# A hybrid decoder layer on one core: the up projection computed by channels, with the weights as left operand and the norm's factor applied to its result

## The chip, the cores and the metric

The kernel runs on one core of one Trainium2 chip. The metric is the device time of one execution in microseconds (us): the median of three runs of the kernel before is 1485.3, and the runs lie between 1483.8 and 1486.86.

## The reference

One layer of a hybrid decoder trunk, for 256 tokens of width 2048, in float32. A state-space group and an attention group work side by side on a normalised input, their outputs go through one output projection, then come a feed-forward network with a convolution in it and a gated embedding. The part that the change touches is the feed-forward network:

```
n       = RMSNorm(h)                       # h / sqrt(mean(h^2) + 1e-6) * gain, per token
[g | u] = causal_dwconv3(n @ W_up)         # 2048 -> 2 x 5632 channels; 3 taps over tokens, per channel, and a bias
h       = h + (SiLU(g) * u) @ W_down       # 5632 -> 2048
h       = h + sigmoid(RMSNorm(h) @ W_pg) * RMSNorm(p @ W_pe)
```

The factor 1 / sqrt(mean(h^2) + 1e-6) is one number per token. It may be applied before or after the product with W_up, since it is the same for all channels; the convolution mixes tokens, so it comes behind the factor.

## The kernel before, in words

**Tiles.** The 256 tokens (T) are two blocks of 128 (NB = 2). Weights come in chunks of 512 output columns (NC = 512), and a chunk with its 2048 rows comes in eight pieces of two row tiles each (KW = 2; 128 x 1024 numbers, 512 KB), each with one DMA on SyncE's queue. `load_w` (L201) makes two tiles of each piece: wh, the high part, by a cast on ScalarE (L195), and wl = w - wh on VectorE (L196). Both are fp32r, the type that TensorE takes here. The activations are kept the same way, as high and low tiles (class `Lhs`, L240), with channels on the partitions. There are four buffers of wh and of wl.

**Products.** `products` (L214) computes, for a piece's two row tiles and the two token blocks, three matmuls each into the block's accumulator (a PSUM bank of 128 tokens x 512 channels): high activations by wh (L231), high by wl (L232), low by wh (L233). The activations are the left operand (the one that TensorE loads, 128 x 128), the weights stream past as the right operand, 512 columns a matmul. A chunk of the up projection has 16 row tiles x 2 blocks x 3 = 96 such matmuls.

**The up projection** (`up`, L781) handles one chunk: the 96 matmuls (`gemm`, L783), a copy of the two accumulators that is scaled by the norm's factor rh (one number per token, and so per partition; ScalarE, L787), and `conv_chunk` (L284). The convolution runs along tokens, so the chunk is first turned by eight transposes on TensorE (L291) into two PSUM tiles; from there `conv_tile` (L275) makes the last tap with the bias on ScalarE (L278) and adds the two others on VectorE (L280). There are 22 chunks, 11 of g and 11 of u, in turn. SiLU is on ScalarE, the product g * u on GpSimd (L803), and the split of the result on ScalarE and VectorE. The down projection (`project`, L382) of a segment of chunk pairs (segments of 2, 2, 2, 2, 2 and 1 pairs) comes one segment later.

**Ahead of it.** The last output projection (`project` with `next_lhs`, L747) adds its chunks to the residual h and at once prepares the next left operand hT: ScalarE squares and sums h (L374), and `transpose_split` (L257) turns h with 16 transposes a chunk (L264) into two PSUM tiles and writes the high part, times the norm's gain (gain: per channel), on ScalarE (L198) and the low part on VectorE (L199). `finish_rstd` (L377) sums the squares (L379) and makes rh with a multiply and add (L188) and a power on GpSimd (L190). Then the layer's embedding input pT and the convolution's weights fcw are loaded on ScalarE's queue (L756, L763), and pT is split into ph and pl (L764). hT uses the same SBUF tiles as the left operand aT before it.

**Behind it.** The last down projection prepares h2T in the same way (L810), then come the embedding product (L811) and the gate (L821 to L832).

**PSUM.** Three pools of two buffers each are open for the whole kernel: the accumulator pairs (ps_acc, 4 banks), the turned tiles (ps_tr, 2) and the rest (ps_ms, 2): all eight banks.

**What sets the order.** The program is written in the order above, but a list scheduler with a model of the engines reorders it: each engine gets its own stream of instructions, and runs it strictly in order. So a matmul that is written early may stand later in TensorE's stream, and in the streams transposes stand among the matmuls of the next step. The scheduler's choice is fixed when the kernel is built. A buffer is taken when its earlier readers are done; a pool that is opened in place of a closed one waits in the same way.

Of the kernel before, what the change touches and what calls it, by code (L numbers as in the profile page):

```python
# [11 lines left out]
F32 = mybir.dt.float32  # L12
F32R = mybir.dt.float32r
I32 = mybir.dt.int32
AF = mybir.ActivationFunctionType
ALU = mybir.AluOpType
AX = mybir.AxisListType
PSUM = bass.MemoryType.PSUM

P = 128  # L20
T = 256
# [4 lines left out]
NC = 512  # L26
# [38 lines left out]
def hybrid_layer(  # L65
# [29 lines left out]
    ps_acc = ctx.enter_context(tc.tile_pool(name="ps_acc", bufs=2, space=PSUM))  # L95
    ps_tr = ctx.enter_context(tc.tile_pool(name="ps_tr", bufs=2, space=PSUM))
    ps_ms = ctx.enter_context(tc.tile_pool(name="ps_ms", bufs=2, space=PSUM))
# [3 lines left out]
    def nm(s):  # L101
        uid[0] += 1
        return f"{s}_{uid[0]}"
# [15 lines left out]

    def acc_pair():  # L120
        return [ps_acc.tile([P, NC], F32, tag=f"acc{b}", name=nm(f"acc{b}")) for b in range(NB)]

    def tr_tile():
        return ps_tr.tile([P, NC], F32, tag="tr", name=nm("tr"))
# [115 lines left out]
    class Lhs:  # L240


        def __init__(self, pool, kt, tag):
            self.t = [
                (sb(pool, [P, KG, T], f"{tag}h{g}", F32R), sb(pool, [P, KG, T], f"{tag}l{g}", F32R))
                for g in range((kt + KG - 1) // KG)
            ]

        def part(self, k):
            h, l = self.t[k // KG]  # L250
            return h[:, k % KG, :], l[:, k % KG, :]

# [117 lines left out]
    def next_lhs(lhs, ss, n, gain):  # L370

        for b in range(NB):
            sq = sb(small, [P, NC], "hsq")
            S.activation(out=sq, in_=hres[b][:, n * NC : (n + 1) * NC], func=AF.Square, accum_out=ss[:, b, n : n + 1])  # L374
        transpose_split([hres[b][:, n * NC : (n + 1) * NC] for b in range(NB)], lhs, 4 * n, gain)
# [374 lines left out]
    mix.close()  # L750

# [27 lines left out]
    with tc.tile_pool(name="ffn", bufs=2) as fp:  # L779

        def up(c):  # L781
            acc = acc_pair()
            gemm(acc, hT, [w_up[c, g] for g in range(KT // KW)])  # L783
            t = []
            for b in range(NB):
                u_ = sb(fp, [P, NC], f"u{b}")
                S.activation(out=u_, in_=acc[b], func=AF.Copy, scale=rh[:, b : b + 1])  # L787
                t.append(u_)
            cv = sb(fp, [P, 4, T], f"cv{c // NPAIR}")
            conv_chunk(t, cv, fcw, 3, 4 * c)  # L790
            return cv
# [108 lines left out]
```

## Time and profile before

| what | value |
|---|---|
| median of three runs | 1485.3 us (1483.8 to 1486.86) |
| the profiled execution's own time | 1484.0 us |
| its span in the trace | 1482.3 us |
| TensorE, matmuls (PE) | 1472.4 us busy, 99% of the span |
| TensorE, weight loads (PEld) | 1199.1 us busy, 81% |
| VectorE (DVE) | 961.8 us busy, 65% |
| ScalarE (ACT) | 799.9 us busy, 54% |
| GpSimd (POOL) | 155.2 us busy, 10% |
| DMA | 271.65 MB, mean 183 GB/s |

How to read the profile's lines: a busy time is the time in which an engine had an instruction under way. Matmuls are pipelined, so two of them overlap, and their pace is read from their starts and not from their durations. A row of groups gives the program's line, the engine, the operation, the tiles (out<-in), shapes and count, then the sum in us and the mean of one in ns, then the idle time of the engine ahead of them and what ended it. A row of the timeline gives the start in us from the span's start, the duration in us, the engine, the line, the instruction with its tiles and shape, and a count where several follow each other; brackets behind it name a wait and what ended it. A row of windows gives a stretch and, for PE, PEld, DVE, ACT and POOL in that order, the busy time with the number of instructions (ahead of them, the sum of PE's), then the granted clock of TensorE, the share of DMA and the GB/s. A "q" behind an engine's name is its DMA queue.

### The profile page before, as it was taken

To read this page: it belongs to the slowest core of one execution; us is meant where nothing else is said; L and a number is where in the kernel's file an instruction comes from. 1 tells how busy PE (TensorE), PEld (TensorE's weight loads), DVE (VectorE), ACT (ScalarE), POOL (GpSimd) and SP (SyncE) were. 2 spreads that over 40 slices of the span, in tenths; PEclk is the share of its full clock that TensorE was granted. 3 is DMA by queue.
4 is the path that set the end of the run, shared out by engine and by line. 5 is a ranking of instruction groups with operands and counts; after the bars stand their busy time and mean duration, and the time that the engine had idled before them with its cause. 6 is when DMAs were issued, how large, how long until landed. Compare 5 with 4: busy or idle time off the path is not lost.

```text
span 1482.3 us, 18476 instructions
## 1 busy us (share of the span) xinstructions
PE 1472.4 (99%) x6836; PEld 1199.1 (81%) x6836; DVE 961.8 (65%) x1264; ACT 799.9 (54%) x1111; POOL 155.2 (10%) x148
## 2 busy tenths in 40 slices
PE   9999999999999999999999999999999999999998
PEld 7787888888777777788888888888888888888887
DVE  7578776656768687766556646565665556566854
ACT  7575555645555554566555545544543554454643
POOL 1004022034033030000000000000000000000000
PEclk9999999999999999999999999999999999999999
DMA  9665655655555555466666666666666665666673
GB/s 344 187 200 171 203 183 160 185 155 172 157 156 150 164 146 160 132 191 204 184 187 186 186 193 185 187 190 191 182 192 191 184 193 186 187 190 188 208 222 100
DMA packets 79098, 271.65 MB, mean 183 GB/s; under 512 B 8752, under 2 KB 11504, under 8 KB 78624
## 3 DMA queue, kind: packets, MB, share of 16 engines
q1 hardware_dynamic: 78176, 269.55, 59.8%
q8 instruction: 53, 0.87, 0.2%
q10 hardware_dynamic: 720, 0.74, 0.1%
q0 software_dynamic: 112, 0.19, 0.1%
q14 instruction: 37, 0.30, 0.1%
HBM read 268.32 MB, written 2.13 MB: 182 GB/s over the span
## 4 chain that ended last, share of the span: by engine, by line
PE 93%; DVE 2%; DMA 2%; POOL 2%; issue 1%; ACT 1%; SPq 0%; DVEq 0%; POOLq 0%
PE acc L231 26%; PE acc L232 26%; PE acc L233 26%; PE acc L223 5%; PE tr L291 2%; PE ms L656 1%; PE ms L505 1%; DMA seg<-scr 1%; PE ms L697 1%; PE tr L264 1%; PE tr L689 1%; DVE wl L196 1%; DMA w<-in_w_in_dram 1%; PE acc L330 1%; PE acc L331 1%
## 5 line engine op out<-in xcount | busy, mean ns | idle before, releaser
L196 DVE TENSOR_TENSOR wl<-w,wh 128x1024 fp32r<-128x1024 f32 (+1 forms) x493 | 616.5, 1253 | 406.8 <-ACT wh L195 405.1
L195 ACT CAST wh<-w 128x1024 fp32r<-128x1024 f32 (+1 forms) x493 | 516.8, 1050 | 484.7 <-PE acc L233 382.0
L232 PE MATMUL acc<-wl,ah 128*128 128x512 f32 x1168 | 457.1, 391 | 0.8 <-DVE wl L196 0.5
L231 PE MATMUL acc<-wh,ah 128*128 128x512 f32 x1168 | 457.5, 393 | 0.0
L233 PE MATMUL acc<-wh,al 128*128 128x512 f32 x1168 | 457.3, 393 | 0.0
L232 PEld LDWEIGHTS acc<-wl,ah 128*128 128x128 f32 x1168 | 219.4, 188 | 47.7 <-DVE wl L196 2.1
L231 PEld LDWEIGHTS acc<-wh,ah 128*128 128x128 f32 x1168 | 219.5, 188 | 45.7 <-issue 1.8
L233 PEld LDWEIGHTS acc<-wh,al 128*128 128x128 f32 x1168 | 219.0, 188 | 44.8 <-issue 0.8
L231 PE MATMUL acc<-wh,gh 128*128 128x512 f32 x352 | 137.5, 391 | 0.0
L233 PE MATMUL acc<-wh,gl 128*128 128x512 f32 x352 | 137.5, 391 | 0.0
L232 PE MATMUL acc<-wl,gh 128*128 128x512 f32 x352 | 137.1, 389 | 0.0
L803 POOL TENSOR_TENSOR cv<-cv,cv 128x1024 f32<-128x1024 f32 x11 | 35.8, 3254 | 648.4 <-DVE cv L280 562.8
L231 PE MATMUL acc<-wh,yh 128*128 128x512 f32 x256 | 101.1, 397 | 0.0
L232 PE MATMUL acc<-wl,yh 128*128 128x512 f32 x256 | 100.6, 393 | 0.0
L233 PE MATMUL acc<-wh,yl 128*128 128x512 f32 x256 | 100.5, 395 | 0.0
L280 DVE SCALAR_TENSOR_TENSOR cv<-tr,fcw,cv 128x254 f32<-128x254 f32 (+1 forms) x176 | 74.0, 475 | 19.3 <-ACT cv L278 19.3
L368 DVE TENSOR_TENSOR h<-h,acc 128x512 f32<-128x512 f32 x112 | 73.7, 680 | 11.1 <-PE acc L233 11.1
L233 PEld LDWEIGHTS acc<-wh,gl 128*128 128x128 f32 x352 | 66.1, 188 | 13.5
L232 PEld LDWEIGHTS acc<-wl,gh 128*128 128x128 f32 x352 | 66.1, 188 | 13.5
L231 PEld LDWEIGHTS acc<-wh,gh 128*128 128x128 f32 x352 | 66.1, 188 | 13.3
L278 ACT ACTIVATE cv<-tr,fcw 128x256 f32<-128x256 f32 x88 | 44.9, 561 | 34.1 <-PE tr L291 34.1
L231 PEld LDWEIGHTS acc<-wh,yh 128*128 128x128 f32 x256 | 48.1, 188 | 12.0 <-issue 2.1
(240 smaller groups left out, 1282.9 us busy)
## 6 DMA issues: line engine op xcount, KB each, us to landing
w<-in_w_up_dram SPq DMA_DIRECT2D x176, 512.0 KB, 3.9
w<-in_w_in_dram SPq DMA_DIRECT2D x127, 512.0 KB, 3.7
w<-in_w_down_dram SPq DMA_DIRECT2D x88, 512.0 KB, 3.7
w<-in_w_out_dram SPq DMA_DIRECT2D x64, 512.0 KB, 3.7
w<-in_w_pg_dram SPq DMA_DIRECT2D x32, 512.0 KB, 4.3
seg<-scr SPq DMA_DIRECT2D x8, 512.0 KB, 6.0
h<-in_x_dram SPq DMA_DIRECT2D x2, 1024.0 KB, 8.3
w<-in_w_pe_dram SPq DMA_DIRECT2D x4, 512.0 KB, 3.7
```

The source lines that it names most:

```text
L195: S.copy(hi, src)
L196: V.tensor_tensor(out=lo, in0=src, in1=hi.bitcast(F32), op=ALU.subtract)
L223: PE.matmul(acc[b], lhsT=l, rhs=r, start=(k == 0 and m == 0), stop=(k == total - 1 and m == 2))
L231: PE.matmul(acc[b], lhsT=hi, rhs=wh[:, i, :], start=(k == 0), stop=False)
L232: PE.matmul(acc[b], lhsT=hi, rhs=wl[:, i, :], start=False, stop=False)
L233: PE.matmul(acc[b], lhsT=lo, rhs=wh[:, i, :], start=False, stop=(k == total - 1))
L264: PE.transpose(tr[:, i, b * P : (b + 1) * P], src[b][:, f * P : (f + 1) * P], ident)
L278: S.activation(out=dst, in_=ps, func=AF.Identity, scale=taps[n - 1], bias=bias)
L280: V.scalar_tensor_tensor(out=dst[:, s:], in0=ps[:, : T - s], scalar=taps[n - 1 - s], in1=dst[:, s:], op0=ALU.mult, op1=ALU.add)
L291: PE.transpose(tr[:, i, b * P : (b + 1) * P], src[b][:, f * P : (f + 1) * P], ident)
L368: V.tensor_tensor(out=hs, in0=hs, in1=acc[b], op=ALU.add)
L803: G.tensor_tensor(out=cg, in0=cg, in1=cu, op=ALU.mult)
```

## The change

In words:

- **One PSUM pool from there on.** When rh has been made, the three pools are closed and one pool ps_b is opened, of four tags with two buffers each: again eight banks. `acc_pair` and `tr_tile` take their tiles from it in turn. The embedding, the gate and the down projection use it too.
- **High and low activations side by side.** `Lhs` now holds one tile for each group with the high 256 tokens and the low 256 next to each other, so that one right operand can span both (`pair`, 512 columns).
- **The up projection by channels.** `up` uses the weights as left operand: for each row tile and each of four groups of 128 channels, one long product, wh by the high and low activations (512 columns, L823 of the kernel after), and one short one, wl by the high activations (256 columns, L821). They go in rows of four, long then short, for the second row tile of a piece short then long. Each of the four banks holds 128 channels x 256 tokens of the high products in its left half (the wl products should land with one of the halves: they go to the right half, `acc[f][:, T:]`) and the low ones in its right half. A chunk has 64 long and 64 short products. Its result has channels on the partitions already, so the eight transposes of a chunk go.
- **The norm's factor behind the product.** rh has one number per token, and tokens now lie along a row. So rt, a tile of 128 partitions x 256 tokens with the factor in each partition, is made once by two matmuls with the identity (L803) and a copy (L804). For each chunk ScalarE copies the four left halves (L827), VectorE adds the four right halves (L828) and multiplies all four by rt in one instruction (L829). Then `conv_tile` works as before, from SBUF in place of PSUM.

The diff:

```diff
--- before
+++ after
@@ -92,9 +92,11 @@
     act = ctx.enter_context(tc.tile_pool(name="act", bufs=1))
     const = ctx.enter_context(tc.tile_pool(name="const", bufs=1))
     small = ctx.enter_context(tc.tile_pool(name="small", bufs=2))
-    ps_acc = ctx.enter_context(tc.tile_pool(name="ps_acc", bufs=2, space=PSUM))
-    ps_tr = ctx.enter_context(tc.tile_pool(name="ps_tr", bufs=2, space=PSUM))
-    ps_ms = ctx.enter_context(tc.tile_pool(name="ps_ms", bufs=2, space=PSUM))
+    banks = ExitStack()
+    ps_acc = banks.enter_context(tc.tile_pool(name="ps_acc", bufs=2, space=PSUM))
+    ps_tr = banks.enter_context(tc.tile_pool(name="ps_tr", bufs=2, space=PSUM))
+    ps_ms = banks.enter_context(tc.tile_pool(name="ps_ms", bufs=2, space=PSUM))
+    ps_b = []
 
     uid = [0]
 
@@ -117,10 +119,22 @@
         if n:
             G.memset(sb(pool, [P, n // 4], "fill", bufs=1), 0.0)
 
+    def bank(i):
+
+        return ps_b[0].tile([P, NC], F32, tag=f"b{i}", name=nm(f"bank{i}"))
+
+    took = [0, 0]
+
     def acc_pair():
+        if ps_b:
+            took[0] ^= 2
+            return [bank(took[0] + b) for b in range(NB)]
         return [ps_acc.tile([P, NC], F32, tag=f"acc{b}", name=nm(f"acc{b}")) for b in range(NB)]
 
     def tr_tile():
+        if ps_b:
+            took[1] = (took[1] + 1) % 4
+            return bank(took[1])
         return ps_tr.tile([P, NC], F32, tag="tr", name=nm("tr"))
 
     def ms_tile():
@@ -241,14 +255,15 @@
 
 
         def __init__(self, pool, kt, tag):
-            self.t = [
-                (sb(pool, [P, KG, T], f"{tag}h{g}", F32R), sb(pool, [P, KG, T], f"{tag}l{g}", F32R))
-                for g in range((kt + KG - 1) // KG)
-            ]
+            self.both = [sb(pool, [P, KG, 2, T], f"{tag}{g}", F32R) for g in range((kt + KG - 1) // KG)]
+            self.t = [(t[:, :, 0, :], t[:, :, 1, :]) for t in self.both]
 
         def part(self, k):
             h, l = self.t[k // KG]
             return h[:, k % KG, :], l[:, k % KG, :]
+
+        def pair(self, k):
+            return self.both[k // KG][:, k % KG, :, :]
 
         def __call__(self, k, b):
             h, l = self.part(k)
@@ -372,6 +387,7 @@
         for b in range(NB):
             sq = sb(small, [P, NC], "hsq")
             S.activation(out=sq, in_=hres[b][:, n * NC : (n + 1) * NC], func=AF.Square, accum_out=ss[:, b, n : n + 1])
+
         transpose_split([hres[b][:, n * NC : (n + 1) * NC] for b in range(NB)], lhs, 4 * n, gain)
 
     def finish_rstd(ss, tag):
@@ -748,6 +764,8 @@
 
     rh = finish_rstd(ssh, "rh")
     mix.close()
+    banks.close()
+    ps_b.append(ctx.enter_context(tc.tile_pool(name="ps_b", bufs=2, space=PSUM)))
 
 
     pp = ctx.enter_context(tc.tile_pool(name="pe", bufs=1))
@@ -778,16 +796,40 @@
 
     with tc.tile_pool(name="ffn", bufs=2) as fp:
 
+
+        rt = sb(fp, [P, T], "rt", bufs=1)
+        tr = tr_tile()
+        for b in range(NB):
+            PE.matmul(tr[:, b * P : (b + 1) * P], lhsT=rh[:, b : b + 1].to_broadcast([P, P]), rhs=ident, start=True, stop=True)
+        S.copy(rt, tr[:, :T])
+
         def up(c):
-            acc = acc_pair()
-            gemm(acc, hT, [w_up[c, g] for g in range(KT // KW)])
-            t = []
-            for b in range(NB):
-                u_ = sb(fp, [P, NC], f"u{b}")
-                S.activation(out=u_, in_=acc[b], func=AF.Copy, scale=rh[:, b : b + 1])
-                t.append(u_)
+
+
+
+
+            acc = [bank(f) for f in range(4)]
+            for s in range(KT // KW):
+                wh, wl = load_w(w_up[c, s])
+                for i in range(KW):
+                    k = s * KW + i
+                    hl = hT.pair(k)
+                    for m in ((0, 1), (1, 0))[i]:
+                        for f in range(4):
+                            fs = slice(f * P, (f + 1) * P)
+                            if m:
+                                PE.matmul(acc[f][:, T:], lhsT=wl[:, i, fs], rhs=hl[:, 0, :], start=False, stop=False)
+                            else:
+                                PE.matmul(acc[f], lhsT=wh[:, i, fs], rhs=hl, start=(k == 0), stop=(k == KT - 1))
             cv = sb(fp, [P, 4, T], f"cv{c // NPAIR}")
-            conv_chunk(t, cv, fcw, 3, 4 * c)
+            u_ = sb(fp, [P, 4, T], "u")
+            for f in range(4):
+                S.copy(u_[:, f, :], acc[f][:, :T])
+                V.tensor_tensor(out=u_[:, f, :], in0=u_[:, f, :], in1=acc[f][:, T:], op=ALU.add)
+            V.tensor_tensor(out=u_, in0=u_, in1=rt.unsqueeze(1).to_broadcast([P, 4, T]), op=ALU.mult)
+            for f in range(4):
+                w = fcw[:, (4 * c + f) * 4 : (4 * c + f + 1) * 4]
+                conv_tile(u_[:, f, :], cv[:, f, :], [w[:, j : j + 1] for j in range(3)], w[:, 3:4])
             return cv
 
         pair = 0
```

The scheduler moves instructions at the passage from the last output projection to the up projection, and behind the first up chunk. In the rows below a name such as wh_1216 is a tile, with the program's number of it; the left operand of a matmul stands behind the arrow with the right one.

First TensorE at the passage. Before: the last matmul of the output projection (yl0 is its left operand), then the up projection (ah0 and al0 are hT, high and low, acc0 and acc1 the two token blocks) and, eleven rows behind, the first of the last 24 transposes of h:

```order
L233 MATMUL acc1_1187_5621<-wh_1192_5641,yl0_1044_4953 128x512
L231 MATMUL acc0_1213_5714<-wh_1216_5717,ah0_507_2628 128x512
L231 MATMUL acc1_1214_5715<-wh_1216_5717,ah0_507_2628 128x512
L232 MATMUL acc0_1213_5714<-wl_1217_5718,ah0_507_2628 128x512
L233 MATMUL acc0_1213_5714<-wh_1216_5717,al0_508_2629 128x512
L232 MATMUL acc1_1214_5715<-wl_1217_5718,ah0_507_2628 128x512
L233 MATMUL acc1_1214_5715<-wh_1216_5717,al0_508_2629 128x512
L231 MATMUL acc0_1213_5714<-wh_1216_5717,ah0_507_2628 128x512
L232 MATMUL acc0_1213_5714<-wl_1217_5718,ah0_507_2628 128x512
L231 MATMUL acc1_1214_5715<-wh_1216_5717,ah0_507_2628 128x512
L232 MATMUL acc1_1214_5715<-wl_1217_5718,ah0_507_2628 128x512
L264 MATMUL tr_1172_5540<-ident_10_114,h0_1_84 128x128
```

After, on the same engine: the end of those 24 transposes (which all stand directly behind the last matmul of the output projection), the two matmuls that spread rh, and then the up projection's first rows:

```order
L279 MATMUL tr_1181_5657<-ident_10_114,h0_1_84 128x128
L279 MATMUL tr_1181_5657<-ident_10_114,h1_2_85 128x128
L279 MATMUL tr_1181_5657<-ident_10_114,h0_1_84 128x128
L279 MATMUL tr_1181_5657<-ident_10_114,h1_2_85 128x128
L803 MATMUL bank1_1193_5700<-ident_10_114,rh_1184_5672 128x128 x2
L823 MATMUL bank0_1197_5707<-a0_499_2620,wh_1202_5712 128x512
L823 MATMUL bank1_1198_5708<-a0_499_2620,wh_1202_5712 128x512
L823 MATMUL bank2_1199_5709<-a0_499_2620,wh_1202_5712 128x512
L823 MATMUL bank3_1200_5710<-a0_499_2620,wh_1202_5712 128x512
L821 MATMUL bank0_1197_5707<-a0_499_2620,wl_1203_5713 128x256
L821 MATMUL bank1_1198_5708<-a0_499_2620,wl_1203_5713 128x256
L821 MATMUL bank2_1199_5709<-a0_499_2620,wl_1203_5713 128x256
```

What moved: the 24 transposes, which stood among the first up matmuls, now stand ahead of all of them, and the two matmuls that read rh stand between.

Next VectorE at the same place. Before: the sum of squares (L379), low halves of hT (L199), rh's multiply and add (L188), splits of weights (wl) and pl:

```order
L379 TENSOR_REDUCE s1_1198_5684<-ssh_515_2636 128x2
L199 SCALAR_TENSOR_TENSOR al1_510_2631<-tr_1172_5540,gains_3_92,ah1_509_2630 128x256
L188 TENSOR_SCALAR rs_t_1199_5686<-s1_1198_5684 128x2
L196 TENSOR_TENSOR wl_1229_5790<-w_1227_5788,wh_1228_5789 128x1024
L196 TENSOR_TENSOR pl_1206_5701<-pe0_1201_5694,ph_1205_5700 128x512
L199 SCALAR_TENSOR_TENSOR al1_510_2631<-tr_1172_5540,gains_3_92,ah1_509_2630 128x256
L199 SCALAR_TENSOR_TENSOR al1_510_2631<-tr_1173_5549,gains_3_92,ah1_509_2630 128x256
L196 TENSOR_TENSOR wl_1232_5808<-w_1230_5806,wh_1231_5807 128x1024
```

After, the same with the kernel after's lines (L395 for L379, L213 for L199, L202 for L188, L210 for L196):

```order
L213 SCALAR_TENSOR_TENSOR a1_500_2621<-tr_1157_5533,gains_3_92,a1_500_2621 128x256
L395 TENSOR_REDUCE s1_1182_5668<-ssh_503_2624 128x2
L213 SCALAR_TENSOR_TENSOR a1_500_2621<-tr_1156_5524,gains_3_92,a1_500_2621 128x256
L202 TENSOR_SCALAR rs_t_1183_5670<-s1_1182_5668 128x2
L210 TENSOR_TENSOR pl_1190_5691<-pe0_1185_5684,ph_1189_5690 128x512
L213 SCALAR_TENSOR_TENSOR a1_500_2621<-tr_1157_5533,gains_3_92,a1_500_2621 128x256
L213 SCALAR_TENSOR_TENSOR a2_501_2622<-tr_1168_5586,gains_3_92,a2_501_2622 128x256
L213 SCALAR_TENSOR_TENSOR a2_501_2622<-tr_1169_5595,gains_3_92,a2_501_2622 128x256
```

What moved: pl stands between two low halves of the first pair of tiles, as before, but the low half behind it (of tile tr_1157) now has to be done before TensorE's next transposes and with them all up matmuls.

Last VectorE behind the first up chunk, after: two splits of weights, the four adds, the multiply, a third split and the taps:

```order
L210 TENSOR_TENSOR wl_1236_5939<-w_1234_5937,wh_1235_5938 128x1024
L210 TENSOR_TENSOR wl_1239_5961<-w_1237_5959,wh_1238_5960 128x1024
L828 TENSOR_TENSOR u_1226_5888<-u_1226_5888,bank0_1197_5707 128x256
L828 TENSOR_TENSOR u_1226_5888<-u_1226_5888,bank1_1198_5708 128x256
L828 TENSOR_TENSOR u_1226_5888<-u_1226_5888,bank2_1199_5709 128x256
L828 TENSOR_TENSOR u_1226_5888<-u_1226_5888,bank3_1200_5710 128x256
L829 TENSOR_TENSOR u_1226_5888<-u_1226_5888,rt_1192_5699 128x1024
L210 TENSOR_TENSOR wl_1242_5983<-w_1240_5981,wh_1241_5982 128x1024
```

In the kernel before, splits of weights stand at this place, and behind them the taps, which read the turned tiles.

Over the whole program 176 transposes of chunks go from TensorE, 2112 matmuls of 512 columns go, and 1408 long and 1408 short products come, with the two that spread rh.

## The prediction

> **What bounds the kernel now.** I read the page first, then the stages by windows, then the up projection's matmuls in order of time.
>
> ```profile
> PE 1472.4 (99%) x6836; PEld 1199.1 (81%) x6836; DVE 961.8 (65%) x1264; ACT 799.9 (54%) x1111; POOL 155.2 (10%) x148
> PE 93%; DVE 2%; DMA 2%; POOL 2%; issue 1%; ACT 1%; SPq 0%; DVEq 0%; POOLq 0%
> ```
>
> TensorE is busy all the time and carries 93% of the chain that ended last; VectorE and ScalarE have a third and more to spare. The windows are from the first up matmul to the first down projection, that projection, and the next four up chunks; the last row is the transposes alone in the third window.
>
> ```profile
> 634.17:817.63 183.46, 183.46 (x849) 152.03 (x848) 113.33 (x141) 105.29 (x132) 10.53 (x5) 1.00 0.63 190
> 817.63:862.08 44.45, 44.45 (x201) 36.83 (x200) 28.30 (x32) 20.34 (x22) 3.23 (x1) 1.00 0.64 190
> 862.08:951.90 89.82, 89.82 (x409) 74.43 (x408) 51.29 (x59) 47.11 (x54) 3.22 (x1) 1.00 0.63 188
> 862.08:951.90 89.82, 3.58 (x24) 2.97 (x24) 1.00 0.63 188
> ```
>
> PE's busy time equals each window: in the up stage nothing but PE's own pace counts. Busy time says nothing of that pace, since the matmuls overlap; starts do.
>
> ```profile
> 799.72 0.39 PE L233 MATMUL acc<-wh,al 128*128 128x512 f32 x1
> 799.95 0.82 PE L291 MATMUL tr<-ident,u 128*128 128x128 f32 x6
> 801.06 0.39 PE L233 MATMUL acc<-wh,al 128*128 128x512 f32 x1
> 801.99 0.39 PE L231 MATMUL acc<-wh,ah 128*128 128x512 f32 x1
> 803.81 0.39 PE L233 MATMUL acc<-wh,al 128*128 128x512 f32 x1
> ```
>
> From 801.99 to 803.81 are eight matmuls of 512 columns: 0.2275 us from start to start. From 799.72 to 801.06 are three of them (L233, L231, L232) and six transposes: (1.34 - 3 x 0.227) / 6 = 0.110 us a transpose. The third window, four chunks of 96 matmuls and 24 transposes, gives the pace closer: (89.82 - 24 x 0.110) / 384 = 0.2270 us. So an up chunk costs PE 96 x 0.2270 + 8 x 0.110 = 22.67 us, and there are 22.
>
> **The change, part by part.**
>
> *Products.* A chunk now has 64 long products (512 columns: high and low half of the activations against wh) and 64 short ones (256 columns against wl), 128 weight loads in place of 96, and no transposes. The columns streamed are the same: 64 x 512 + 64 x 256 = 96 x 512. A long product costs what it does now. A short one with 128 weight columns isn't in the trace; its neighbours are
>
> ```profile
> 53.80 0.28 PE L347 MATMUL ms<-ah,dhl 128*64 128x256 f32 x1
> 54.97 0.28 PE L347 MATMUL ms<-ah,dhl 128*64 128x256 f32 x1
> 254.16 0.60 PE L465 MATMUL ms<-CT,BT 128*128 128x128 f32 x4
> L465 PE MATMUL ms<-CT,BT x16: 270/274/275, 104.6 to 254.5; 128*128 128x128 f32 x16
> L465 PEld LDWEIGHTS ms<-CT,BT x16: 187/190/192, 104.4 to 254.4; 128*128 128x128 f32 x16
> ```
>
> The first two rows are ten steps apart: fp32r products of 256 columns with 64 or 32 weight columns, 1.17 / 10 = 0.117 us each. The third is a run of four fp32 products, each with its own 128-column load: (0.60 - 0.27) / 3 = 0.110 us, so a load that is recorded with 190 ns hides behind a product and can follow each 0.110 us. That is the lower end. For the upper end I take the long product's whole overhead: the kernel's first matmuls, at what looks like half clock, start each
>
> ```profile
> 1.82 3.60 PE L156 MATMUL ms<-warm 128*128 128x512 bf16 x8 [1.82 <-POOL warm L139]
> 3.93 1.49 PE L156 MATMUL ms<-warm 128*128 128x512 bf16 x3
> 5.61 2.05 PE L329 MATMUL acc<-wh,ah 128*128 128x512 f32 x4 [0.19 <-ACT wh L195]
> 7.45 0.82 PE L330 MATMUL acc<-wl,ah 128*128 128x512 f32 x2
> ```
>
> (3.93 - 1.82) / 5 = 0.422 us, so 512 columns stream in some 0.211 us at full clock, the overhead is 0.016 us, and a short product costs at most 0.106 + 0.016 = 0.122 us. I take 0.1185, between 0.117 (same columns and type) and the 0.120 to 0.122 of the same weights. A chunk then takes 64 x 0.2270 + 64 x 0.1185 = 22.11 us: 0.56 us less, 12.3 us over 22. The ends: 0.117 gives 14.3 us, 0.122 7.3 us.
>
> *Evacuation.* It gets longer on VectorE but is covered. Durations of like rows:
>
> ```profile
> L657 DVE TENSOR_TENSOR s<-ms,band 128x256 f32<-128x256 f32 x16 | 6.2, 417 | 4.0 <-PE ms L656 3.9
> L196 DVE TENSOR_TENSOR wl<-w,wh 128x1024 fp32r<-128x1024 f32 x491 | 615.1, 1255 | 406.8 <-ACT wh L195 405.1
> L280 DVE SCALAR_TENSOR_TENSOR cv<-tr,fcw,cv 128x255 f32<-128x255 f32 x88 | 39.7, 478 | 19.3 <-ACT cv L278 19.3
> L195 ACT CAST yh<-ms 128x256 fp32r<-128x256 f32 x16 | 6.0, 373 | 20.1 <-PE ms L697 20.1
> L195 ACT CAST wh<-w 128x1024 fp32r<-128x1024 f32 x491 | 515.5, 1051 | 484.0 <-PE acc L233 382.0 <-PE acc L223 34.9 <-issue 22.1
> ```
>
> Per chunk VectorE gets four adds (0.42) and a 1024-wide multiply (1.25) beside its eight splits (10.0) and eight taps (3.8): 16.7 of 22.1 us. ScalarE trades two scaled copies for four small ones. In the order three weight pieces of the next chunk are split ahead of the four adds. After a chunk's last matmul, four copies (1.5), the last add (0.4), the multiply and the fourth split (1.25 each) end after some 4.5 us; PE needs that piece after three pieces, 3 x 22.1 / 8 = 8.3 us. Slack 3.8 us: nothing on the path. The four banks have a second set, so PE doesn't wait for the copies either.
>
> *The passage into the up projection.* Here is the loss. Before, the last 24 transposes of the residual (six tiles) stand between up matmuls and everything that they wait for is hidden:
>
> ```profile
> 633.95 0.39 PE L233 MATMUL acc<-wh,yl 128*128 128x512 f32 x1
> 634.17 0.62 PE L231 MATMUL acc<-wh,ah 128*128 128x512 f32 x2
> 634.37 0.34 ACTq L756 DMA_DIRECT2D fcw<-in_ffn_cw_dram  x1
> 634.86 0.34 ACTq L763 DMA_DIRECT2D pe<-in_pT_dram  x1
> 636.38 0.62 ACT L374 ACTIVATE hsq<-h 128x512 f32<-128x512 f32 x1
> 639.32 0.62 ACT L195 CAST ph<-pe 128x512 fp32r<-128x512 f32 x1 [0.72 <-DMA pe<-in_pT_dram]
> 639.97 0.69 DVE L196 TENSOR_TENSOR pl<-pe,ph 128x512 fp32r<-128x512 f32 x1
> 652.45 0.60 PE L264 MATMUL tr<-ident,h 128*128 128x128 f32 x4
> L198 ACT ACTIVATE ah<-tr,gains 128x256 fp32r<-128x256 f32 x32 | 14.6, 470 | 8.9 <-PE tr L264 8.8
> L199 DVE SCALAR_TENSOR_TENSOR al<-tr,gains,ah 128x256 fp32r<-128x256 f32 x32 | 14.8, 478 | 4.5 <-ACT ah L198 4.5
> ```
>
> Now the first bank of the new pool takes the place of old banks, all of them must be read out, and the 24 transposes and the two matmuls that spread rh stand ahead of the first up matmul. PE works through them in turns with ScalarE and VectorE, two tiles at a time, as two buffers allow. From 634.17: four transposes, 0.60, then ScalarE's copy and square, so that pT's load (the page shows it 4.46 us from issue to ph) is issued at about 635.9, not 634.86; ph starts at 640.4 and ends at 641.0; pl stands on VectorE ahead of the last low half of that pair and ends at 641.7; that half ends at 642.2. Only then is the buffer free for the fourth tile. From there two rounds follow: transposes 0.75 with their start, three copies at some 0.43 each, the last low half 0.5: 2.55 us each, to 647.3. The reciprocal root is long done. The two spreading matmuls need 0.4 us: the first up matmul starts at 647.7, 13.5 us after 634.17. Of that 24 x 0.110 = 2.6 us was paid before too. Loss 10.9 us; if the load lands a microsecond sooner or later, 9.7 to 12.1.
>
> *The clock after the gap.* PE stands still from about 635.1 to 639.6, and again between the rounds. At the kernel's start matmuls were slow from 1.82 to 7.87 us: 13 of them, 0.20 us over their later pace, 2.6 us. I take that, 0 to 3.0 being the ends. The Trainium skill, page "TensorE: Matmul & The Clock Gate", Part 1, says that one idle window of about 3.4 us halves the clock until a busy window has passed. By that rule the gap of 4.5 us may or may not hold a whole window, and the slow time would be worth an estimated 1.7 to 3.4 us.
>
> *The rest* (embedding, gate, output) keeps its order; only banks' names change there: nothing.
>
> **The sum.** 1484.0 (the profiled execution) - 12.3 + 10.9 + 2.6 = 1485.2. The median of the runs is 1.3 above the profiled one: 1486.5. What a measurement of this kernel can tell from no change is 0.2%, 3 us; the forecast, 1.2 above the median, is no change.
>
> **Rivals.**
>
> 1. The clock stays up through the passage, as the transposes and spreading matmuls keep PE active. 1483.9. For it: no idle stretch but the first is over 2.5 us.
>
> 2. A short product goes at the pace of the fp32 run, 0.110 us: a chunk takes 21.57 us, the gain is 24.2 us, and the time 1474.6. For it: 128 columns of fp32 there may well be the same stream as 256 of fp32r. Against: the fp32r row, 0.117.
>
> 3. Slower: loads set the short products' pace, because the next load starts only when a product starts, and the product needs its end. At the recorded 190 ns a chunk is 64 x (0.2270 + 0.190) = 26.69 us, 4.02 more than before: 88 us, and 1587. It decides from 0.127 us a short product on, where a chunk costs as much as before. Against it speaks the run at 0.110. The Trainium skill, same page, section "Back-to-back issue gap", says that pairs of load and product with 128 columns are sustained at about 81 ns against 56 alone. By that ratio a short product would cost an estimated 0.15 us, a chunk 24.4 us, and the kernel some 1524 us; no run here shows bf16 pairs, and the fp32 run speaks against it.
>
> 4. The longer evacuation does reach PE: VectorE waits for ScalarE in each step, and if the 3.8 us of slack go and 1 us more, the chunks lose 22 us: 1508. Against: VectorE is idle a quarter of the time.
>
> **How the numbers follow.** Forecast 0.44, clock stays 0.26, fast short products 0.10, loads 0.07, evacuation 0.06; 0.07 for what I don't see. The likeliest case spans 1481 to 1491 (gain 14.3 and no clock loss, to gain 10 with a late load and 3.0). Down to 1476 it takes in a part of rival 2; rivals 3 and 4 stay out. Faster by over 0.2%: rival 2, a third of rival 1 and a little of the forecast and of the unseen, 0.23. Slower: rivals 3 and 4, a quarter of the forecast, part of the unseen, 0.28. The rest, 0.49, is no change.
>
> **What would show it.** Right: starts of short products 0.117 to 0.122 us apart; an up chunk of 22.0 to 22.3 us without idle time; PE without an up matmul for 12 to 15 us after the last output projection, with pT's load, ph and pl in the chain of waits; matmuls 0.43 us apart for some microseconds behind it. Wrong: short products over 0.127, idle time of PE before wl in each chunk, or a passage of under 6 us.

## The result and the profile after

The changed kernel takes 1490.38 us (median of 6 runs, 1489.51 to 1493.4), the kernel before 1485.07 in its 6 runs: a ratio of 1.0037, interval 1.0026 to 1.0048. It is slower by 5.3 us, which is more than the 0.2% that tell from no change. The forecast was 1486.5, "no change", with a likeliest case of 1481 to 1491.

The page of the changed kernel: busy times, and the chain that ended last by engine.

```profile
PE 1469.4 (99%) x7368; PEld 1221.2 (82%) x7368; DVE 1025.4 (69%) x1374; ACT 795.5 (53%) x1156; POOL 156.8 (11%) x148
PE 92%; DVE 2%; DMA 2%; POOL 2%; issue 1%; ACT 1%; SPq 0%; DVEq 0%; POOLq 0%
```

Nothing here says that the kernel got slower: TensorE is busy 3 us less, still 99%. The difference lies in stages. The windows are the first eight up chunks, the first down projection, the next four up chunks, and the passage from the last output projection to the first up matmul:

```profile
649.04:829.32 180.28, 180.28 (x1026) 158.61 (x1026) 123.95 (x158) 96.55 (x130) 9.71 (x3) 0.99 0.59 181
829.32:872.85 43.53, 43.53 (x194) 36.05 (x192) 31.55 (x37) 20.39 (x24) 3.21 (x1) 1.00 0.63 193
872.85:962.23 89.38, 89.38 (x513) 78.66 (x512) 59.53 (x75) 46.20 (x61) 3.23 (x1) 1.00 0.62 189
634.63:649.04 14.41, 6.00 (x30) 4.67 (x28) 9.22 (x19) 7.93 (x18) 0.83 (x2) 0.63 0.45 160
```

An up chunk takes 89.38 / 4 = 22.345 us, without idle time. It was 22.67, so 22 chunks give 7.2 us. The passage takes 14.41 us with TensorE busy in 6.00 of them, at a clock of 0.63; before there was none. Its rows in the timeline of TensorE:

```profile
634.40 0.39 PE L247 MATMUL acc<-wh,y 128*128 128x512 f32 x1
634.63 1.03 PE L279 MATMUL tr<-ident,h 128*128 128x128 f32 x8
639.55 1.09 PE L279 MATMUL tr<-ident,h 128*128 128x128 f32 x4 [3.88 <-DVE rs_t L202]
641.40 1.09 PE L279 MATMUL tr<-ident,h 128*128 128x128 f32 x4 [0.77 <-DVE a L213]
644.05 1.94 PE L279 MATMUL tr<-ident,h 128*128 128x128 f32 x8 [1.57 <-DVE a L213]
648.19 1.19 PE L803 MATMUL bank<-ident,rh 128*128 128x128 f32 x4 [2.20 <-DVE a L213]
649.04 2.05 PE L823 MATMUL bank<-a,wh 128*128 128x512 f32 x4
650.89 1.69 PE L821 MATMUL bank<-a,wl 128*128 128x256 f32 x8
652.41 2.00 PE L823 MATMUL bank<-a,wh 128*128 128x512 f32 x8
```

Eight transposes take 1.03 us ahead of the idle 3.88 us, and behind it 1.94: half speed. The first four long products start (650.89 - 649.04) / 4 = 0.46 us apart, twice their 0.23, and from 652.41 on the pace is back.

So the 6.1 us between the two profiled spans (1482.3 and 1488.4) are made up like this: the first up matmul starts 649.04 - 634.17 = 14.87 us later, of which the 24 transposes, 2.64, were paid behind it before: +12.2. Of these, 0.45 are no part of the passage, since the last output matmul already starts at 634.40 in place of 633.95; the passage itself loses 14.41 - 2.64 = 11.8. The slow start of the first chunk: 180.28 - 8 x 22.345 = +1.5. The chunks: -7.2. All the rest: -0.4.

### The profile page after: what moved, and what is told of

Read it like the earlier page. It is cut to its first block, busy times and chain, and to the rows that moved or that the text cites. A ratio compares the mean times of both kernels' runs of the same rounds, so it can differ in the third digit from the quotient of the medians.

```text
span 1488.4 us, 19686 instructions
## 1 busy us (share of the span) xinstructions
PE 1469.4 (99%) x7368; PEld 1221.2 (82%) x7368; DVE 1025.4 (69%) x1374; ACT 795.5 (53%) x1156; POOL 156.8 (11%) x148
## 4 chain that ended last, share of the span: by engine, by line
PE 92%; DVE 2%; DMA 2%; POOL 2%; issue 1%; ACT 1%; SPq 0%; DVEq 0%; POOLq 0%
PE bank L823 22%; PE bank L821 11%; PE acc L245 10%; PE acc L246 9%; PE acc L247 9%; PE bank L246 6%; PE bank L245 6%; PE bank L247 6%; PE bank L237 5%; PE ms L672 1%; PE ms L521 1%; PE ms L713 1%; DMA seg<-scr 1%; DVE wl L210 1%; PE tr L705 1%
## 5 line engine op out<-in xcount | busy, mean ns | idle before, releaser
L210 DVE TENSOR_TENSOR wl<-w,wh 128x1024 fp32r<-128x1024 f32 (+1 forms) x493 | 628.4, 1277 | 361.8 <-ACT wh L209 360.2
L823 PE MATMUL bank<-a,wh 128*128 128x512 f32 x1408 | 354.3, 393 | 0.0
L823 PEld LDWEIGHTS bank<-a,wh 128*128 128x128 f32 x1408 | 253.7, 189 | 45.3
L821 PEld LDWEIGHTS bank<-a,wl 128*128 128x128 f32 x1408 | 192.8, 191 | 13.8
L821 PE MATMUL bank<-a,wl 128*128 128x256 f32 x1408 | 196.9, 283 | 0.0
L246 PE MATMUL acc<-wl,a 128*128 128x512 f32 x448 | 176.9, 395 | 0.8 <-DVE wl L210 0.8
L247 PE MATMUL acc<-wh,a 128*128 128x512 f32 x448 | 177.0, 395 | 0.0
L245 PE MATMUL acc<-wh,a 128*128 128x512 f32 x448 | 176.2, 395 | 0.0
L246 PE MATMUL bank<-wl,g 128*128 128x512 f32 x352 | 137.2, 390 | 0.0
L247 PE MATMUL bank<-wh,g 128*128 128x512 f32 x352 | 137.0, 389 | 0.0
L245 PE MATMUL bank<-wh,g 128*128 128x512 f32 x352 | 135.5, 390 | 0.0
L245 PE MATMUL acc<-wh,y 128*128 128x512 f32 x256 | 101.1, 397 | 0.0
L247 PE MATMUL acc<-wh,y 128*128 128x512 f32 x256 | 100.5, 395 | 0.0
L245 PEld LDWEIGHTS acc<-wh,a 128*128 128x128 f32 x448 | 84.2, 188 | 18.9 <-issue 1.8
L247 PEld LDWEIGHTS acc<-wh,a 128*128 128x128 f32 x448 | 84.2, 188 | 17.5 <-issue 0.8
L246 PEld LDWEIGHTS bank<-wl,g 128*128 128x128 f32 x352 | 66.1, 188 | 13.5
```

Source lines behind the costliest of these rows:

```text
L210: V.tensor_tensor(out=lo, in0=src, in1=hi.bitcast(F32), op=ALU.subtract)
L245: PE.matmul(acc[b], lhsT=hi, rhs=wh[:, i, :], start=(k == 0), stop=False)
L246: PE.matmul(acc[b], lhsT=hi, rhs=wl[:, i, :], start=False, stop=False)
L247: PE.matmul(acc[b], lhsT=lo, rhs=wh[:, i, :], start=False, stop=(k == total - 1))
L821: PE.matmul(acc[f][:, T:], lhsT=wl[:, i, fs], rhs=hl[:, 0, :], start=False, stop=False)
L823: PE.matmul(acc[f], lhsT=wh[:, i, fs], rhs=hl, start=(k == 0), stop=(k == KT - 1))
```

## The experiments

### The passage

**The pool change alone.** The kernel before, with only the pool hunks of the change. The one that counts (the others give `acc_pair` and `tr_tile` their banks):

```diff
     mix.close()
+    banks.close()
+    ps_b.append(ctx.enter_context(tc.tile_pool(name="ps_b", bufs=2, space=PSUM)))
```

> The kernel before with the one PSUM pool alone (old banks closed, new pool from the up projection on); products, transposes of the chunks and the norm's factor as before. If the pool's closing makes the passage (the theory): the first up matmul starts some 13.4 us after the last output projection matmul, of which 2.6 us are the transposes paid before too; with 1.5 to 2.0 us of slow matmuls behind it the kernel takes 12 to 13 us more, 1497.4. If the two matmuls that spread rh are what holds the passage up (the rival), this kernel has none and stays at 1485 to 1487.

Measured: 1498.91 us beside 1484.85, a ratio of 1.0096 (1.0082 to 1.0110), 14 us more. TensorE's timeline, with rows left out at the dots:

```profile
635.71 0.39 PE L247 MATMUL acc<-wh,yl 128*128 128x512 f32 x1
635.95 1.03 PE L278 MATMUL tr<-ident,h 128*128 128x128 f32 x8
640.86 0.80 PE L278 MATMUL tr<-ident,h 128*128 128x128 f32 x4 [3.88 <-DVE rs_t L202]
...
649.51 0.77 PE L245 MATMUL bank<-wh,ah 128*128 128x512 f32 x1 [2.20 <-DVE al L213]
...
654.77 0.43 PE L245 MATMUL bank<-wh,ah 128*128 128x512 f32 x1
```

From the start of the last output matmul to that of the first up matmul 13.8 us, 13.4 had been expected, with the same idle 3.88 us. In the changed kernel it is 14.64; the 0.84 between are the two matmuls that spread rh, 0.85 us from 648.19 to 649.04. So the closing of the pools makes the passage, and those two only stand in it. The 14 us are above the 12 to 13 that were expected: twelve slow matmuls from 649.51 to 654.77 lose some 2.5 us, where 1.5 to 2.0 had been counted.

**One set of banks from the start.** The changed kernel, with eight banks in one pool for the whole kernel, and the first chunk's four among those that are free by then (the functions that hand out the banks change with it and are left out here):

```diff
-    ps_acc = banks.enter_context(tc.tile_pool(name="ps_acc", bufs=2, space=PSUM))
-    ps_tr = banks.enter_context(tc.tile_pool(name="ps_tr", bufs=2, space=PSUM))
-    ps_ms = banks.enter_context(tc.tile_pool(name="ps_ms", bufs=2, space=PSUM))
+    ps_all = ctx.enter_context(tc.tile_pool(name="ps_all", bufs=1, space=PSUM))
...
-    banks.close()
-    ps_b.append(ctx.enter_context(tc.tile_pool(name="ps_b", bufs=2, space=PSUM)))
+    nxt = took[0] ^ 2
+    sets.extend([(nxt, nxt + 1, 6, 7), (took[0], took[0] + 1, 4, 5)])
```

> The changed kernel with one set of eight banks from the kernel's start in place of closed and reopened pools; the first up chunk takes four banks that are free by then. All else, the two matmuls that spread rh included, as changed. Theory (the passage costs 13.7 us: 12.2 us without an up matmul and 1.5 us of slow ones behind): 1490.4 - 13.7 = 1476.7 us, faster than before by about 8, with up matmuls from 0.23 us behind the last output projection on and a chunk of 22.35 us as in the changed kernel. Rival (the waits for hT's last parts reach PE another way, as the chunk by channels needs every bank from the first row tile on): 1481 to 1490, with idle time of PE in the first chunk.

Measured: 1479.62 us, a ratio of 0.9967 (0.9956 to 0.9979): between the theory's 1476.7 and the rival's 1481 to 1490. The timeline of TensorE, at the kernel's start and at the passage:

```profile
6.49 1.17 PE L347 MATMUL bank<-wh,a 128*128 128x512 f32 x4 [1.07 <-DVE a L335]
11.57 0.74 PE L347 MATMUL bank<-wh,a 128*128 128x512 f32 x2 [2.08 <-ACT a L215]
...
639.22 0.39 PE L250 MATMUL bank<-wh,y 128*128 128x512 f32 x1
639.45 1.07 PE L827 MATMUL bank<-a,wh 128*128 128x512 f32 x4
```

The passage is gone: the first up matmul stands 0.23 us behind the last output matmul, though the matmuls on rh are still there. But that place is reached 5.3 us late, and a part of this shows as waits in the first 12 us, where another bank rotation made another order. So the loss lies ahead of the passage, and the next run leaves that part alone.

**The old pools kept open.** The changed kernel with nothing closed; a chunk takes the accumulator pair and two banks of the other pools in turn. The pool hunks are those of the kernel before again; the one in `up`:

```diff
-            acc = [bank(f) for f in range(4)]
+            more = tr_tile if turns[0] else ms_tile
+            turns[0] ^= 1
+            acc = acc_pair() + [more(), more()]
```

> The changed kernel with the three old PSUM pools kept open to the end; each up chunk takes the accumulator pair and two banks of ms or of tr in turn, so its products, the factor's row and the evacuation are as changed and only the closing of the pools goes. The kernel with one set of banks from the start took 835.9 us from its first up matmul to its last matmul, but that first one stood at 639.45 us, where before it stood at 634.17. Theory (those 5.3 us came from the other bank rotation ahead of the up projection, and not from it): first up matmul at 634.2 us, a chunk of 22.35 us, 1477 us (1475 to 1478.5), which is 8 us less than before. Rival (early up matmuls take the place of other work whichever the pools): first up matmul at 637 to 639 us, 1479 to 1481.

Measured: 1477.62 us beside 1485.86, a ratio of 0.9947 (0.9934 to 0.9959), as the theory had it. The timeline of TensorE, then the window of four up chunks:

```profile
634.32 0.39 PE L233 MATMUL acc<-wh,y 128*128 128x512 f32 x1
634.54 0.62 PE L811 MATMUL acc<-a,wh 128*128 128x512 f32 x2
...
636.41 0.60 PE L265 MATMUL tr<-ident,h 128*128 128x128 f32 x4
636.76 0.70 PE L811 MATMUL acc<-a,wh 128*128 128x512 f32 x2
```

```profile
859.94:949.32 89.38, 89.38 (x513) 78.66 (x512) 59.53 (x75) 46.21 (x61) 3.23 (x1) 1.00 0.60 188
```

The transposes stand among up matmuls again, and a chunk takes its 22.345 us. This is the change without the passage: 8.2 us faster than before. Pools alone, +14 us, and products alone, -8, make the +5.3 of the change within a microsecond.

**pT's load moved.** In the changed kernel's chain of the passage the load stands with 4.11 us:

```profile
635.38 4.11 DMA pe<-in_pT_dram
639.49 0.02 issue
639.51 0.63 ACT ph L209
640.14 0.02 issue
640.17 0.69 DVE pl L210
640.86 0.40 DVE a L213
```

The load goes behind the first up chunk (it is taken out at its old place):

```diff
                 cg = up(pair + i)
+                if pair + i == 0:
+                    nc.scalar.dma_start(pt_, pT)
+                    split(pt_, ph, pl)
```

> The changed kernel with the load of pT and its two splits moved behind the first up chunk in the program; nothing else. In the changed kernel the chain of the passage runs through that load (635.38 to 639.49 us), ph and pl. Theory: ScalarE and VectorE then go on with hT while the load would have been waited for, the second transposes behind the gap start at about 640.0 in place of 641.40: 1.4 us less, 1489.0 (1488.4 to 1489.6). Rival (the whole load is on the path, as the chain has it): 4 us less, 1486.4. Rival (the rounds between TensorE, ScalarE and VectorE set the pace anyway): no change, 1490.4.

Measured: 1490.47 us, a ratio of 1.0030 (1.0018 to 1.0042). This tells nothing on the load, since it did not move. It stands in the chain of the passage as before, with ph and pl behind it:

```profile
635.93 4.69 DMA pe<-in_pT_dram
```

The scheduler put load and splits where they had been. So the next kernel has none. It leaves out the embedding's input, and takes two row tiles of h2T in its place, so a part of its output is of other numbers:

```diff
-    nc.scalar.dma_start(pt_, pT)
-    split(pt_, ph, pl)
...
-            return ph[:, k, b * P : (b + 1) * P], pl[:, k, b * P : (b + 1) * P]
+            return h2T(k, b)
```

> The changed kernel without the load of pT and without its two splits; the embedding's products take two row tiles of h2T in place of ph and pl, so that part of the output is of other numbers. It asks what moving the code was to ask: there the scheduler put load and splits back into the same place. Theory: without ph and pl ScalarE and VectorE go on with hT at once, the second transposes behind the gap start 1.4 us sooner and the first up matmul at 647 to 647.7 us in place of 649.04: 1488.4 to 1489.2. Rival (the load's whole 4.1 us on the path): first up matmul at 645, 1486.3. Rival (the rounds set the pace anyway): 649, 1490.4.

Measured: 1489.49 us, a ratio of 1.0029 (1.0017 to 1.0041), which can't be told from the changed kernel's 1.0037 by time. The trace can. TensorE's timeline:

```profile
639.27 1.94 PE L279 MATMUL tr<-ident,h 128*128 128x128 f32 x8 [3.88 <-DVE rs_t L202]
642.78 1.94 PE L279 MATMUL tr<-ident,h 128*128 128x128 f32 x8 [1.57 <-DVE a L213]
646.92 1.19 PE L798 MATMUL bank<-ident,rh 128*128 128x128 f32 x4 [2.20 <-DVE a L213]
647.76 2.05 PE L818 MATMUL bank<-a,wh 128*128 128x512 f32 x4
```

The first up matmul starts at 647.76 in place of 649.04, 1.28 us sooner. But 0.28 of this come before the passage, which begins at 634.35 here and at 634.63 there: it takes 13.41 us in place of 14.41, so load and splits are worth 1.0 us, and the theory said 1.4. The chain shows the load with 4.11 us, yet the idle 3.88 us of TensorE is there without it too. What the chain has in this time in the kernel without the load:

```profile
635.37 0.71 ACT hsq L389 x2
636.08 0.94 ACT wh L209
637.02 0.02 issue
637.04 1.23 DVE wl L210
```

ScalarE squares h and casts a weight piece, VectorE splits that piece, and only then come the low halves for which TensorE waits. Behind that, the rounds of transpose, copy and low half, two tiles at a time, hold the rest.

### The products

**Long and short in turn.**

```diff
-                    for m in ((0, 1), (1, 0))[i]:
-                        for f in range(4):
+                    for f in range(4):
+                        for m in ((0, 1), (1, 0))[i]:
```

> The changed kernel with long and short products in turn, bank by bank, in place of rows of four (rows of eight with the next row tile's). A chunk takes 22.345 us in the changed kernel, where 64 x 0.2270 + 64 x 0.1185 was forecast, 22.11; the long products of its rows start 0.2304 us apart in the mean. Theory A (a short product costs 0.122 us, a fixed overhead like the long one's, and its late part shows at the next long ones): order doesn't matter, a chunk of 22.3 to 22.4, 1490 us. Theory B (each switch from a row of short ones to long ones costs 27 ns, 8 switches a chunk): 56 switches or so, a chunk of 23.6 us, 1519. Theory C (loads of weights fall behind in the short rows and hide again behind long products when each short one stands beside a long one): a chunk of 21.8 us, 1478.

Measured: 1492.89 us, a ratio of 1.0066 (1.0048 to 1.0084). The window of four up chunks:

```profile
874.05:963.91 89.86, 89.86 (x513) 78.42 (x512) 59.15 (x76) 47.23 (x62) 3.22 (x1) 1.00 0.62 188
```

22.465 us a chunk, 0.12 more. B and C fall. A is not quite right either, as order matters a little.

**All long.**

```diff
-                                PE.matmul(acc[f][:, T:], lhsT=wl[:, i, fs], rhs=hl[:, 0, :], start=False, stop=False)
+                                PE.matmul(acc[f], lhsT=wl[:, i, fs], rhs=hl, start=False, stop=False)
```

> The changed kernel with the short products made long: wl by both halves of the activations, 512 columns, which adds the low by low product that the others leave out. A chunk is 128 long products in rows through four banks. Theories A and C: no short product is left to be paid for, so the long ones start 0.2270 us apart and a chunk takes 29.06 us: 1490.4 + 22 x (29.06 - 22.345) = 1638. Theory D (a long product in this form, weights as left operand and four banks in turn, costs 0.2304 by itself): 29.5 us a chunk, 1648.

Measured: 1638.22 us (one run). The window of four up chunks:

```profile
927.59:1043.64 116.05, 116.05 (x513) 96.13 (x512) 60.11 (x75) 46.26 (x61) 2.40 (x1) 1.00 0.47 146
```

The low by low product comes in with this. 116.05 / 512 = 0.2267 us a product. D falls: the long product in its new form costs what it did.

**All short.** Each long product as two of 256 columns:

```diff
-                                PE.matmul(acc[f], lhsT=wh[:, i, fs], rhs=hl, start=(k == 0), stop=(k == KT - 1))
+                                for z in range(2):
+                                    PE.matmul(acc[f][:, z * T : (z + 1) * T], lhsT=wh[:, i, fs], rhs=hl[:, z, :], start=(k == 0 and z == 0), stop=(k == KT - 1 and z == 1))
```

> The changed kernel with each long product made as two of 256 columns, high and low half apart with the same weights: 192 short products a chunk, 192 loads. With 128 long ones a chunk took 29.01 us, 0.2267 each; with 64 and 64, 22.345, so a short one costs 22.345 - 64 x 0.2268 = 7.83 / 64 = 0.1223. Theory A (that is its own price: 256 columns and the same overhead as any): 192 x 0.1223 = 23.5 us a chunk, starts 0.122 apart, 1490.4 + 22 x 1.14 = 1515. Rival (a short one costs 0.119 as its starts say, and the mixing of the two costs the rest): 22.8 us a chunk, 1501. If the loads, 0.19 us as recorded, set a pace without long products to hide behind: over 24.5 us, over 1537.

Measured: 1507.73 us (one run). The window of four up chunks:

```profile
880.70:972.85 92.15, 92.15 (x769) 92.15 (x768) 59.29 (x75) 46.13 (x61) 3.23 (x1) 1.00 0.55 183
```

92.15 / 768 = 0.1200 us a product, between A's 0.122 and the rival's 0.119. Loads are under way in all of the 92.15 us, and still a short product follows each 0.120 us: a load's recorded 0.19 us sets no pace.

Alone, then, 64 long and 64 short ones cost 64 x (0.2267 + 0.1200) = 22.19 us, and a chunk takes 22.345. The remaining 0.16 us come with the mix. Two kernels vary the rows' length. Rows of sixteen, on the kernel with the old pools:

```diff
-                for i in range(KW):
-                    k = s * KW + i
-                    hl = hT.pair(k)
-                    for m in ((0, 1), (1, 0))[i]:
+                for m in ((0, 1), (1, 0))[s % 2]:
+                    for i in range(KW):
+                        k = s * KW + i
+                        hl = hT.pair(k)
```

> The kernel with the old pools, whose chunk takes 22.345 us like the changed one's, with products in rows of sixteen (all long ones of a piece, then its short ones, the next piece's short ones, its long ones) in place of eight: four turns from short to long a chunk in place of eight. Short ones alone start 0.120 apart and long ones alone 0.2268, which makes 22.195 a chunk; 0.15 us is left. Theory F (each turn costs some 19 ns): a chunk of 22.27, 1.7 us less in all, 1475.9. Rival (the 0.15 us come with the mix, whatever the rows): 22.345, 1477.6.

Measured: 1476.65 us beside 1484.57, a ratio of 0.9942 (0.9929 to 0.9954). The window of four up chunks:

```profile
857.05:946.12 89.07, 89.07 (x513) 78.71 (x512) 57.70 (x75) 46.46 (x61) 3.23 (x1) 1.00 0.61 190
```

Rows of four, on the changed kernel (at a chunk's last row tile the order is turned, so one row of eight short ones remains):

```diff
-                    for m in ((0, 1), (1, 0))[i]:
+                    for m in (0, 1) if k < KT - 1 else (1, 0):
```

> The changed kernel with rows of four in place of eight: sixteen turns a chunk. Theory F (19 ns a turn): a chunk of 22.49 us, 1493.7. Rival (the cost comes with the mix and hardly with the number of turns; with long and short in turn, 56 turns, a chunk took 22.465): between 22.345 and 22.40, 1490.4 to 1491.6.

Measured: 1493.29 us (one run). The window of four up chunks:

```profile
874.67:964.43 89.76, 89.76 (x514) 78.51 (x512) 58.59 (x75) 46.12 (x61) 3.42 (x1) 1.00 0.59 188
```

| rows of | turns from short to long in a chunk | chunk, us | over 22.19, us | for each turn, ns |
|---|---|---|---|---|
| 16 | 4 | 89.07 / 4 = 22.27 | 0.08 | 20 |
| 8 (the change) | 8 | 89.38 / 4 = 22.345 | 0.16 | 20 |
| 4 | 15 | 89.76 / 4 = 22.44 | 0.25 | 17 |
| 1 | 56 | 89.86 / 4 = 22.465 | 0.28 | 5 |

The kernel with rows of four has fifteen turns a chunk, and not the sixteen of its expectation. In rows of eight and more a turn costs 20 ns, so theory F holds there; in shorter rows the cost of a turn falls. The single starts in these traces show where the 20 ns lie. In rows of eight and of sixteen alike, the first five long products behind a turn take 233, 236, 228, 233 and 231 ns to the next start and every later one 227, which is 27 ns too many; the first short one behind long ones takes 113 ns and the second 119 in place of 120, which gives 7 back. A row of four ends before those five are over.

Rows of sixteen on the old pools are the best version that was run, 7.9 us under the kernel before. By time it can't be told from rows of eight (0.9942 and 0.9947, with intervals that overlap); the chunk's 0.08 us can.

## Why the prediction came out as it did

**What bounds the kernel: right.** In each window of chunks TensorE's busy time equals the window, before and after.

**Products: right in direction, wrong in size; this is the term of the sum that was off.** The forecast was "A long product costs what it does now" and "I take 0.1185" for a short one: 22.11 us a chunk, 12.3 us in all. Each form by itself costs 0.2267 and 0.1200; with that second value the gain is some 10.6 us. Together the two prices give (0.2267 - 0.1200) / 256 = 0.417 ns a column and 13 ns a product, beside the 0.211 us for 512 columns (0.412 ns a column) and the 16 ns that the prediction took from the kernel's first matmuls for its upper end. The other 3.4 us go to the turns, 0.16 us x 22, a term that the sum didn't have. Measured is 7.2, the lower end that was named for a short product at 0.122, though the price that brings it there is paid at the long ones. Starts in the changed kernel, in rows of eight:

```profile
673.81 1.11 PE L821 MATMUL bank<-a,wl 128*128 128x256 f32 x8
674.76 2.00 PE L823 MATMUL bank<-a,wh 128*128 128x512 f32 x8
676.60 0.64 PE L821 MATMUL bank<-a,wl 128*128 128x256 f32 x4
```

Eight short ones take 0.95 us, 0.119 each, just what was forecast; the eight long ones behind them 1.84, 0.230 each and not 0.227. Who looks only for "starts of short products 0.117 to 0.122 us apart" finds the forecast confirmed, and the chunk is still 0.24 us longer than it said, just outside its "22.0 to 22.3 us".

**Evacuation: right.** ScalarE's and VectorE's timelines behind a chunk:

```profile
672.40 1.20 ACT L827 COPY u<-bank 128x256 f32<-128x256 f32 x4 [1.04 <-PE bank L823]
```

```profile
672.87 1.41 DVE L828 TENSOR_TENSOR u<-u,bank 128x256 f32<-128x256 f32 x4 [0.26 <-ACT u L827]
674.32 1.23 DVE L829 TENSOR_TENSOR u<-u,rt 128x1024 f32<-128x1024 f32 x1
675.46 1.22 DVE L210 TENSOR_TENSOR wl<-w,wh 128x1024 fp32r<-128x1024 f32 x1
```

Copies, adds, multiply and the fourth split end 676.68 - 672.40 = 4.3 us after they begin; 4.5 was forecast. TensorE has no wait from 655 to 1316 us in the trace, so rival 4 falls.

**The passage: right in its mechanism, somewhat short.** The load was issued at 635.38 us (forecast 635.9), ph began at 639.51 (640.4), pl ended at 640.86 (641.7), the fourth tile's transposes began at 641.40 (642.2). From there to the matmuls on rh it took 6.8 us where 5.1 were forecast. That stretch was counted at full clock and ran at half: its last eight transposes alone take 1.94 us in place of 1.03. The loss was 11.8 us, 10.9 forecast. That the pools and not rh make it, two runs show (the pool change alone, and the old pools kept open); that pT's load is 1.0 us of it, the trace of one. The load holds up the fourth tile, as forecast, and not the third: the 3.88 us of standstill are there without it.

**The clock: right, and put in the wrong place.** It was forecast with 2.6 us, all behind the passage; 1.5 us are there, and it slowed the transposes inside as well. Both terms together were 13.5 in the forecast and are 13.3. Rival 1 (the clock stays up) falls: PEclk is 0.63 in the passage, and 0.50 from 639.55 to 651.90. The rule on the idle window of about 3.4 us in the Trainium skill, page "TensorE: Matmul & The Clock Gate", Part 1, agrees: TensorE stood still for 3.88 us, and what came behind ran at half speed until 652 us.

**The other rivals.** A short product at 0.110 us (rival 2) and one paced by its load (rival 3) both fall with 0.120 in the kernel of short ones alone. The estimate of 0.15 us, from the pairs in the section "Back-to-back issue gap" of the same page of the Trainium skill, doesn't hold for these products of 256 columns in fp32r. The time that the prediction gives with it, 1524, is a slip besides: a chunk of 24.4 us in place of 22.11 adds 50 us to the forecast, which makes some 1537.

In all, the forecast of 1486.5 was 3.9 us low. The sum missed 5.1 us in the products. Passage and clock came out 0.2 lower than forecast, and the step from the profiled execution to the median is 0.2 us, 1.3 forecast; these go the other way. The median lies in the range, but by the prediction's own 0.2% it is slower and not the "no change" that had 0.49; slower had 0.28. That it stayed below 1491 is in part luck: a gain of 7.2 lies outside the 10 that this end allowed, and the slow matmuls behind the passage, 1.5 us where it allowed 3.0, and the smaller step to the median made up for it.

## What to carry to other kernels

The closing of PSUM pools in the middle of this kernel was a wait for all that was in them: alone it cost 14 us, and it ate a gain of 8, and with the old pools kept open the same products made the kernel faster by 0.5%. A stream of mixed instructions is priced by the stage's length divided by its count, and not by the distance between starts of one form, since what one form costs may show at the next. A long entry in the chain of waits isn't what its removal gives, as another path may be nearly as long: the load stood there with 4.1 us and was worth 1.0. A shift between two traces is measured from the start of the stage, and not of the kernel: 0.28 of the 1.28 us came from ahead of it.

## What the runs showed of the hardware

A turn from products of 256 columns to products of 512 costs TensorE 20 ns in rows of eight or sixteen, and less a turn in shorter rows. What causes it stays open: the load's pace by itself is excluded by the kernel of short ones alone, the form of the long ones by the kernel of long ones alone, and the change between wl and wh by both, since both have it and start every 0.120 and 0.227 us. Not settled in detail either are the 5.3 us that one pool from the start lost ahead of the up projection.
